# A third seven-product unit pair in the first panel pairs of the down projection, with deeper rings for the weights' parts

## The chip, the cores and the metric

The kernel runs on one core of one Trainium2 chip. The metric is the device time of one execution in microseconds, as a median of several runs. The profile is that of one execution; its span runs from the first to the last instruction. TensorE is called PE, its weight loads PEld, VectorE DVE, ScalarE ACT, GpSimd POOL; SP is the engine that only issues transfers.

## The reference, cut to what matters

Two layers work on 256 tokens of width 2048, in float32. Layer 0 mixes with gated linear attention, layer 1 with forgetting attention; both also attend to 256 memory tokens. Each layer ends in a gated feed-forward network with a causal convolution over three tokens:

```python
def conv_ffn(h, w_up, conv_w, conv_b, w_down):
    u = causal_dwconv(h @ w_up, conv_w, conv_b)      # h: (256, 2048), w_up: (2048, 11264)
    a, val = split_cols(u, [FFN_HIDDEN, FFN_HIDDEN])
    return (jax.nn.silu(a) * val) @ w_down           # w_down: (5632, 2048)
```

The change lies in `@ w_down`, in both layers, and in the buffers that all projections share.

## The kernel before, in words

**Exact products from three.** Every float32 operand is split into a rounded high part and the rest: `hi` by a ScalarE copy to float32r, `lo = raw - hi` by a VectorE subtraction. A product of two operands is then three matmuls: high by high, low by high, high by low. The activations are split once and stay in SBUF (tiles A and B, 16 chunks of 128 features). The weights come from HBM as they are used.

**Units and rings.** A weight panel is 512 output columns wide. It is cut into units of two chunks of 128 inputs, so a unit is a tile of 128 x 1024 values, 512 KB. A unit passes three rings of tiles: `raw` (four tiles, filled by a transfer that SP issues), `whi` (three, written by ScalarE) and `wlo` (three, written by VectorE). A tile is free again when its last reader is done: `raw` after the subtraction, `whi` after its last matmul with the high part, `wlo` after the last with the low part. `split_unit` and `load_unit` (lines 197 to 219) do this for an ordinary unit: line 207 issues the transfer, line 208 casts, line 217 subtracts. `products` (lines 221 to 233) issues its twelve matmuls: two halves of the tokens, two chunks, three products.

**Seven products in place of eight.** `proj_seven` (lines 270 to 370) computes two panels at once. For one place u in the sum, the two chunks, the two token halves and the two panels form a 2 by 2 block product of eight block products; ordinary unit pairs do all eight, 24 matmuls. For the places listed in `forms`, a Strassen-like form needs seven, 21 matmuls. It needs weight sums (`t13`, `t24`, four VectorE operations on lines 346 to 349, one tile each, not doubled), a half tile (`vhi`, `vlo`) and token sums, the "forms", which `token_sums` makes from the activations beforehand. Four of the seven products go to PSUM banks of their own (`ps_t`, two `ps_s`, `ps_o`), and `more` adds them to the residual stream behind the pair. `halves` (line 307) casts (line 314) and subtracts (line 315) for such a unit, `load` fetches its raw tile; both use the same rings. All matmuls of `proj_seven` are issued by `emit` on line 291.

**The feed-forward network** (`ffn`) goes in three parts of 16, 16 and 12 hidden chunks. In a part, the up panels are computed one after the other, each giving two chunks; its result is written to HBM in turned order, read back (tile `u`), passed through the convolution and the gate in `taken`, and split. Then the down projection of the part runs as four panels, in the first two parts as two pairs, each eight places long. `SEVEN` names the places with the seven-product form in the first and the second pair; `LAST` is the same for the third part and empty.

```python
SEVEN = ((3, 5), (3, 5, 7))
...
for f, at in zip((0, 2), SEVEN):
    add_seven(key, f, m, {u: form(forms[u]) for u in at}, spare_tile)
```

Places are counted from 0 here: 3, 5 and 7 are the 4th, 6th and 8th. `taken` makes the forms of the places for which a tile is held, as soon as the place's two chunks are there.

**What sets the order.** The queues' order is chosen while the program is built, by a planner that runs a timeline of its own. Loads, casts and subtractions of weights have priority over the rest (`AHEAD`), so they run ahead of TensorE as far as the rings let them. Steps such as writing, reading back and convolving are counted in units (`later`, `passed`) and stand behind the cast of that unit in ScalarE's order. [...]

Of the kernel before, what the change touches and what calls it, by code (L numbers as in the profile page):

```python
# [12 lines left out]
F32 = mybir.dt.float32  # L13
F32R = mybir.dt.float32r
# [5 lines left out]
P = 128  # L20
# [11 lines left out]
PARTS = ((0, 16), (16, 32), (32, 44))  # L32
# [4 lines left out]
NVER = 96  # L37
NUNIT = 1024
AHEAD = 300
SEVEN = ((3, 5), (3, 5, 7))  # L40
LAST = ()

SPREAD = [128 * q + 32 * k + i for k in range(4) for i in range(32) for q in range(4)]

WARM = 8

FV_PARTS = ((0, 376), (376, 764), (764, 1152), (1152, 1536))

# [89 lines left out]
def _trunk(ctx: ExitStack, tc: tile.TileContext, xt, xtok, memt, wp, wgu, gns, gfin, cnv, par, msk, out):  # L138
    nc = tc.nc
    where, _ = _layout()  # L140
# [3 lines left out]
    wpool = ctx.enter_context(tc.tile_pool(name="wpool", bufs=4))  # L144
# [25 lines left out]
    with tc.high_priority(offset=2 * AHEAD):  # L170
        V.memset(bufB[KC - 1].bitcast(F32), 0.0)
        warm = pwork.tile([P, 512], F32, name="ps_o", tag="o", bufs=1)
        for i in range(WARM):
            TE.matmul(warm, bufB[KC - 1][:, 0, :P], bufB[KC - 1], start=i == 0, stop=i == WARM - 1)

# [7 lines left out]
    def passed():  # L183

        for d in due:
            d[0] -= 1
        for d in [d for d in due if d[0] == 0]:
            due.remove(d)
            with tc.issue_after(casts[-1].ins):
                d[1]()  # L190
# [6 lines left out]
    def load_unit(unit, pieces=1, before=None, pool=wpool):  # L197
        off, kcs, n = unit
        w = len(kcs) * n
        raw = wpool.tile([P, NUNIT], F32, name="raw", tag="raw", bufs=4)  # L200
        hi = pool.tile([P, NUNIT], F32R, name="whi", tag="whi", bufs=3)
        src = wp[off : off + P * w].rearrange("(p n) -> p n", p=P)
        for i in range(pieces):
            if before is not None:
                before(i)
            s = slice(i * w // pieces, (i + 1) * w // pieces)
            loads.append(nc.sync.dma_start(raw[:, s], src[:, s]))
            casts.append(S.activation(hi[:, s], raw[:, s], AF.Copy))  # L208
        return raw, hi, w

    def split_unit(unit, pieces=1, before=None, pool=wpool):
        with tc.high_priority(offset=AHEAD):
            raw, hi, w = load_unit(unit, pieces, before, pool)
            lo = pool.tile([P, NUNIT], F32R, name="wlo", tag="wlo", bufs=3)
            for i in range(pieces):
                s = slice(i * w // pieces, (i + 1) * w // pieces)
                V.tensor_tensor(lo[:, s], raw[:, s], hi[:, s].bitcast(F32), ALU.subtract)  # L217
        passed()
        return hi, lo
# [50 lines left out]
    def proj_seven(keys, src, forms, evacs, tiles, more, early=False):  # L270

        units = [where[k] for k in keys]
        count, n = len(units[0]), units[0][0][2]
        base = min(min(u[1]) for u in units[0])
        acc = [[pacc.tile([P, 512], F32, name="acc", tag="acc") for _ in range(2)] for _ in keys]
        begun, calls = set(), {}
        shared = []

        def form(a, x, hi, lo, c):
            s = slice(c * n, (c + 1) * n)  # L280
            out = []
            for xs, w in ((x[0], hi), (x[1], hi), (x[0], lo)):
                out.append((a, xs, w[:, s]))
            return out

        def emit(groups):
            todo = [g[n] for n in range(2) for g in groups] + [g[2] for g in groups]
            for a, x, w in todo:
                k = id(a)
                calls[k] -= 1  # L290
                TE.matmul(a[:, :n], x, w, start=k not in begun, stop=calls[k] == 0)  # L291
                begun.add(k)

        def count_calls(a, n):
            calls[id(a)] = calls.get(id(a), 0) + n

        plain = [u for u in range(count) if u not in forms]
        for i in range(2):
            for b in range(2):
                count_calls(acc[i][b], 6 * len(plain))  # L300
        for a in (acc[0][0], acc[1][0], acc[0][1]):
            count_calls(a, 3 * len(forms))

        def token(kc, b):
            return [src[kc - base][:, i, b * P : (b + 1) * P] for i in range(2)]

        def halves(raw, single=False):
            w = n if single else 2 * n
            if single:
                hi, lo = (tiles(t, F32R) for t in ("vhi", "vlo"))  # L310
            else:
                hi, lo = (wpool.tile([P, NUNIT], F32R, name=t, tag=t, bufs=3) for t in ("whi", "wlo"))
            hi, lo = hi[:, :w], lo[:, :w]
            casts.append(S.activation(hi, raw, AF.Copy))  # L314
            V.tensor_tensor(lo, raw, hi.bitcast(F32), ALU.subtract)
            return hi, lo

        def load(unit):
            off, kcs, n = unit
            w = len(kcs) * n  # L320
            raw = wpool.tile([P, NUNIT], F32, name="raw", tag="raw", bufs=4)[:, :w]
            loads.append(nc.sync.dma_start(raw, wp[off : off + P * w].rearrange("(p n) -> p n", p=P)))
            return raw

        for u in range(count):
            k0, k1 = units[0][u][1]
            if u not in forms:
                for i in range(2):
                    hi, lo = split_unit(units[i][u])
                    emit([form(acc[i][b], token(kc, b), hi, lo, c) for b in range(2) for c, kc in enumerate((k0, k1))])  # L330
                    if u == count - 1:
                        for b in range(2):
                            evacs[i](b, acc[i][b][:, :n])
                if u == count - 2 and count - 1 in forms:
                    evacs[1](1, acc[1][1])
                continue
            if not shared:
                shared += [work(t, m) for t, m in (("t", 1), ("s", 2), ("o", 1), ("s", 2))]
                for a in shared:
                    count_calls(a, 3 * len(forms))  # L340
            m1, m5, m6, m7 = shared
            s = forms[u]
            with tc.high_priority(offset=AHEAD + 40):
                r0, r1 = (load(units[i][u]) for i in range(2))
                t13, t24 = (tiles(t, F32)[:, : 2 * n] for t in ("t13", "t24"))
                V.tensor_tensor(t13[:, :n], r1[:, :n], r0[:, :n], ALU.subtract)
                V.tensor_tensor(t13[:, n:], r1[:, n:], r1[:, :n], ALU.subtract)
                V.tensor_tensor(t24[:, :n], r1[:, n:], t13[:, :n], ALU.subtract)
                V.tensor_tensor(t24[:, n:], r0[:, n:], t24[:, :n], ALU.subtract)  # L349
            with tc.high_priority(offset=AHEAD):  # L350
                v0 = halves(r0)
                v1 = halves(r1[:, n:], True)
            passed()
            emit([form(m1, token(k0, 0), *v0, 0), form(acc[0][0], token(k1, 0), *v0, 1)])
            emit([form(acc[1][0], s(3), *v1, 0)])
            with tc.high_priority(offset=AHEAD):
                v2 = halves(t13)
            emit([form(m5, s(0), *v2, 0), form(m7, s(2), *v2, 1)])
            with tc.high_priority(offset=AHEAD):
                v3 = halves(t24)  # L360
            passed()
            emit([form(m6, s(1), *v3, 0), form(acc[0][1], token(k1, 1), *v3, 1)])
            if u == count - 1:
                for i, b in ((0, 0), (1, 0), (0, 1)):
                    evacs[i](b, acc[i][b])
            if early and u == max(forms):
                more(m1, m5, m6, m7)

        if not early:
            more(m1, m5, m6, m7)  # L370
# [692 lines left out]
    def ffn(l, nx, h, m, then, ending=None):  # L1063
        with tc.tile_pool(name=f"ffn{l}", bufs=1) as fp, ExitStack() as ends:
# [3 lines left out]
            sp = sums.enter_context(tc.tile_pool(name=f"sums{l}", bufs=1))  # L1068
# [3 lines left out]
            for u in us:  # L1072
                nc.gpsimd.memset(u[:, :, :2], 0.0)
            turn = [0]
            tiles = [sp.tile([P, 2, 4, P], F32R, name=f"forms{i}") for i in range(3)]
            held = []

            def spare_tile(name, dtype):
# [45 lines left out]

                return evac

            parts = {lo: dict(zip(SEVEN[1] if p < len(PARTS) - 1 else LAST, tiles)) for p, (lo, _) in enumerate(PARTS)}
            for p, (lo, hi) in enumerate(PARTS):
                forms = parts[lo]
                js = list(range(lo, hi, 2))  # L1130
# [6 lines left out]
                if p < len(PARTS) - 1:  # L1137
                    for f, at in zip((0, 2), SEVEN):
                        add_seven(key, f, m, {u: form(forms[u]) for u in at}, spare_tile)
# [33 lines left out]
    n, then, _ = preparing("ffn0", bufB)  # L1173
# [4 lines left out]
    n, then, _ = preparing("ffn1", bufA)  # L1178
# [41 lines left out]
    def closing(ends):  # L1220
        op = ends.enter_context(tc.tile_pool(name="store", bufs=1))
        made["y"] = op.tile([P, 2, 512], F32, name="y")
        return op

    ffn(1, n, bufA, bufB, None, (opened, closing))


# [83 lines left out]
```

## Time and profile before

| | |
|---|---|
| median of 3 runs | 2241.3 us (2240.88 to 2243.91) |
| the profiled execution, span | 2241.1 us |
| matmuls | 10267, PE busy 2227.2 us (99%) |
| VectorE, ScalarE busy | 1658.5 us (74%), 1294.0 us (58%) |
| transfers | 516.98 MB, mean 231 GB/s |
| mean granted TensorE clock | 0.999 |

On one core the span is nearly all of an execution: the profiled one lies inside the spread of the timed runs. A line of the groups view reads: source line, engine, operation, tile written <- tiles read, shape, count | busy time, mean ns of one | idle time of the engine just before, and what ended it. A line of the waits reads: who waited <- for whom: us in total, times, longest. A line of a timeline reads: start, length, engine, source line, operation, tiles, count, and in brackets the idle time before and what ended it.

### The profile page before, as it was taken

The numbers are of one execution on the slowest core, as the hardware profiler recorded it, in microseconds if no ns is written. First come the engines' busy times: TensorE is split into PE (matmuls) and PEld (weight loads), VectorE is DVE, ScalarE is ACT, GpSimd is POOL, SyncE is SP. The second block draws the span as 40 slices with busy tenths as digits, with TensorE's granted clock in tenths as the row PEclk, the third lists the DMA queues.
The fourth block names the chain that finished last, engine by engine and source line by source line (L and its number), as shares of the span: only waits on it lengthen the run. The fifth ranks groups of instructions, "written<-read, shape, count | busy, mean of one in ns | idle before, by whom it ended". The sixth has DMA issues, their size and how long they took to land.

```text
span 2241.1 us, 29637 instructions
## 1 busy us (share of the span) xinstructions
PE 2227.2 (99%) x10267; PEld 1860.8 (83%) x10267; DVE 1658.5 (74%) x2608; ACT 1294.0 (58%) x1921; POOL 44.6 (2%) x71
## 2 busy tenths in 40 slices
PE   9999999999999999999999999999999999999998
PEld 7888888888888888888888898888888888888886
DVE  7568887667689677886777875666778967787766
ACT  7555665656565465555656655555665555554654
POOL 0000000000000000000000000000000000000000
PEclk9999999999999999999999999999999999999999
DMA  9875667677875778667778777677876677767784
GB/s 319 277 234 188 205 208 224 202 234 242 256 222 201 243 233 249 213 203 246 235 254 263 243 239 222 196 233 244 255 243 220 204 239 244 240 193 233 237 242 150
DMA packets 276894, 516.98 MB, mean 231 GB/s; under 512 B 149884, under 2 KB 158600, under 8 KB 276616
## 3 DMA queue, kind: packets, MB, share of 16 engines
q1 hardware_dynamic: 124296, 427.24, 58.9%
q10 hardware_dynamic: 149760, 80.51, 12.6%
q0 software_dynamic: 2688, 7.34, 1.1%
q8 instruction: 80, 1.31, 0.2%
q14 instruction: 70, 0.57, 0.1%
HBM read 470.44 MB, written 44.58 MB: 230 GB/s over the span
## 4 chain that ended last, share of the span: by engine, by line
PE 95%; DMA 3%; DVE 1%; issue 1%; ACT 0%; SPq 0%; DVEq 0%; ACTq 0%
PE acc L229 24%; PE acc L230 24%; PE acc L233 24%; PE acc L291 16%; PE ps_s L291 1%; DMA back<-xturned 1%; PE ps_o L291 1%; PE ps_t L291 1%; DMA back<-turned 1%; DMA raw<-wp 1%; PE ps_s L833 0%; DMA turned<-square 0%; PE ps_s L634 0%; PE ps_t L623 0%; PE ps_o L645 0%
## 5 line engine op out<-in xcount | busy, mean ns | idle before, releaser
L217 DVE TENSOR_TENSOR wlo<-raw,whi 128x1024 fp32r<-128x1024 f32 (+4 forms) x763 | 912.6, 1199 | 458.0 <-ACT whi L208 429.5
L208 ACT ACTIVATE whi<-raw 128x1024 fp32r<-128x1024 f32 (+4 forms) x763 | 791.2, 1040 | 704.7 <-PE acc L230 471.9
L229 PE MATMUL acc<-whi,B 128*128 128x512 f32 (+3 forms) x1440 | 548.1, 382 | 0.0
L230 PE MATMUL acc<-whi,B 128*128 128x512 f32 (+3 forms) x1440 | 547.9, 382 | 0.0
L229 PE MATMUL acc<-whi,A 128*128 128x512 f32 x1120 | 437.3, 392 | 1.7 <-ACT whi L208 1.4
L230 PE MATMUL acc<-whi,A 128*128 128x512 f32 x1120 | 435.4, 390 | 0.0
L233 PE MATMUL acc<-wlo,B 128*128 128x512 f32 (+3 forms) x1440 | 377.0, 381 | 0.0
L229 PEld LDWEIGHTS acc<-whi,B 128*128 128x128 f32 x1440 | 270.3, 188 | 46.9
L230 PEld LDWEIGHTS acc<-whi,B 128*128 128x128 f32 x1440 | 269.9, 188 | 46.3
L233 PEld LDWEIGHTS acc<-wlo,B 128*128 128x128 f32 x1440 | 267.7, 188 | 46.4
L233 PE MATMUL acc<-wlo,A 128*128 128x512 f32 x1120 | 300.6, 390 | 0.3 <-DVE wlo L217 0.3
L229 PEld LDWEIGHTS acc<-whi,A 128*128 128x128 f32 x1120 | 210.3, 188 | 48.1 <-ACT whi L208 3.6
L233 PEld LDWEIGHTS acc<-wlo,A 128*128 128x128 f32 x1120 | 210.1, 188 | 44.3 <-DVE wlo L217 0.7
L230 PEld LDWEIGHTS acc<-whi,A 128*128 128x128 f32 x1120 | 210.3, 188 | 43.5 <-DVE A L527 0.2
L291 PE MATMUL acc<-whi,B 128*128 128x512 f32 x508 | 132.2, 390 | 0.0
L291 PE MATMUL acc<-whi,A 128*128 128x512 f32 x496 | 129.9, 390 | 0.0
L291 PEld LDWEIGHTS acc<-whi,B 128*128 128x128 f32 x508 | 95.1, 188 | 20.3
L1092 ACT ACTIVATE cv<-u,cw 128x256 f32<-128x256 f32 x176 | 96.8, 588 | 23.9 <-DMA u<-turned 23.9
L291 PEld LDWEIGHTS acc<-whi,A 128*128 128x128 f32 x496 | 93.1, 188 | 19.9
L314 ACT ACTIVATE whi<-t 128x1024 fp32r<-128x1024 f32 x46 | 48.9, 1062 | 79.2 <-DVE t L349 42.7
L1093 DVE SCALAR_TENSOR_TENSOR cv<-u,cw,cv 128x256 f32<-128x256 f32 x176 | 78.5, 479 | 15.6 <-ACT cv L1092 15.6
L438 DVE STREAM_TRANSPOSE square<-scaled 128x512 f32<-128x512 f32 x122 | 80.3, 692 | 0.0
(259 smaller groups left out, 1819.5 us busy)
## 6 DMA issues: line engine op xcount, KB each, us to landing
raw<-wp SPq DMA_DIRECT2D x743, 512.0 KB, 4.2
turned<-square ACTq DMA_DIRECT2D x61, 512.0 KB, 4.5
u<-turned ACTq DMA_DIRECT2D x176, 128.0 KB, 5.2
raw<-wp SPq DMA_DIRECT2D x32, 384.0 KB, 3.2
raw<-wp SPq DMA_DIRECT2D x24, 388.0 KB, 3.9
xturned<-square ACTq DMA_DIRECT2D x12, 512.0 KB, 4.3
back<-xturned ACTq DMA_DIRECT2D x40, 128.0 KB, 5.6
raw<-wp SPq DMA_DIRECT2D x8, 400.0 KB, 3.8
```

Source lines behind the costliest of these rows:

```text
L208: casts.append(S.activation(hi[:, s], raw[:, s], AF.Copy))
L217: V.tensor_tensor(lo[:, s], raw[:, s], hi[:, s].bitcast(F32), ALU.subtract)
L229: TE.matmul(acc[:, :n], xh, hi[:, s], start=first and j == 0, stop=False)
L230: TE.matmul(acc[:, :n], xl, hi[:, s], start=False, stop=False)
L233: TE.matmul(a, xh, ls, start=False, stop=stop)
L291: TE.matmul(a[:, :n], x, w, start=k not in begun, stop=calls[k] == 0)
L314: casts.append(S.activation(hi, raw, AF.Copy))
L438: V.transpose(self.square[:, :, :, b], src.rearrange("p (c t) -> p c t", t=32))
L1092: S.activation(r, v[:, 2:], AF.Identity, bias=w[3], scale=w[2])
L1093: V.scalar_tensor_tensor(r, v[:, 1 : T + 1], w[1], r, ALU.mult, ALU.add)
```

## The change

The first pair of the first two down parts gets the seven-product form at a third place, index 1, beside 3 and 5; the second pair keeps its three. A fourth tile for token forms is held, and `SUMS` names the places for which forms are made. The rings become five `raw`, four `whi` and four `wlo` tiles for all projections that use the common pool. The scratch area of the transfers that POOL issues is set to 4096 bytes.

```diff
--- before.py
+++ after.py
@@ -37,12 +37,15 @@
 NVER = 96
 NUNIT = 1024
 AHEAD = 300
-SEVEN = ((3, 5), (3, 5, 7))
+SEVEN = ((1, 3, 5), (3, 5, 7))
+SUMS = (1, 3, 5, 7)
 LAST = ()
 
 SPREAD = [128 * q + 32 * k + i for k in range(4) for i in range(32) for q in range(4)]
 
 WARM = 8
+RING = {"raw": 5, "whi": 4, "wlo": 4}
+SCRATCH = 4096
 
 FV_PARTS = ((0, 376), (376, 764), (764, 1152), (1152, 1536))
 
@@ -197,8 +200,8 @@
     def load_unit(unit, pieces=1, before=None, pool=wpool):
         off, kcs, n = unit
         w = len(kcs) * n
-        raw = wpool.tile([P, NUNIT], F32, name="raw", tag="raw", bufs=4)
-        hi = pool.tile([P, NUNIT], F32R, name="whi", tag="whi", bufs=3)
+        raw = wpool.tile([P, NUNIT], F32, name="raw", tag="raw", bufs=RING["raw"])
+        hi = pool.tile([P, NUNIT], F32R, name="whi", tag="whi", bufs=RING["whi"] if pool is wpool else 3)
         src = wp[off : off + P * w].rearrange("(p n) -> p n", p=P)
         for i in range(pieces):
             if before is not None:
@@ -211,7 +214,7 @@
     def split_unit(unit, pieces=1, before=None, pool=wpool):
         with tc.high_priority(offset=AHEAD):
             raw, hi, w = load_unit(unit, pieces, before, pool)
-            lo = pool.tile([P, NUNIT], F32R, name="wlo", tag="wlo", bufs=3)
+            lo = pool.tile([P, NUNIT], F32R, name="wlo", tag="wlo", bufs=RING["wlo"] if pool is wpool else 3)
             for i in range(pieces):
                 s = slice(i * w // pieces, (i + 1) * w // pieces)
                 V.tensor_tensor(lo[:, s], raw[:, s], hi[:, s].bitcast(F32), ALU.subtract)
@@ -309,7 +312,7 @@
             if single:
                 hi, lo = (tiles(t, F32R) for t in ("vhi", "vlo"))
             else:
-                hi, lo = (wpool.tile([P, NUNIT], F32R, name=t, tag=t, bufs=3) for t in ("whi", "wlo"))
+                hi, lo = (wpool.tile([P, NUNIT], F32R, name=t, tag=t, bufs=RING[t]) for t in ("whi", "wlo"))
             hi, lo = hi[:, :w], lo[:, :w]
             casts.append(S.activation(hi, raw, AF.Copy))
             V.tensor_tensor(lo, raw, hi.bitcast(F32), ALU.subtract)
@@ -318,7 +321,7 @@
         def load(unit):
             off, kcs, n = unit
             w = len(kcs) * n
-            raw = wpool.tile([P, NUNIT], F32, name="raw", tag="raw", bufs=4)[:, :w]
+            raw = wpool.tile([P, NUNIT], F32, name="raw", tag="raw", bufs=RING["raw"])[:, :w]
             loads.append(nc.sync.dma_start(raw, wp[off : off + P * w].rearrange("(p n) -> p n", p=P)))
             return raw
 
@@ -1072,7 +1075,7 @@
             for u in us:
                 nc.gpsimd.memset(u[:, :, :2], 0.0)
             turn = [0]
-            tiles = [sp.tile([P, 2, 4, P], F32R, name=f"forms{i}") for i in range(3)]
+            tiles = [sp.tile([P, 2, 4, P], F32R, name=f"forms{i}") for i in range(len(SUMS))]
             held = []
 
             def spare_tile(name, dtype):
@@ -1124,7 +1127,7 @@
 
                 return evac
 
-            parts = {lo: dict(zip(SEVEN[1] if p < len(PARTS) - 1 else LAST, tiles)) for p, (lo, _) in enumerate(PARTS)}
+            parts = {lo: dict(zip(SUMS if p < len(PARTS) - 1 else LAST, tiles)) for p, (lo, _) in enumerate(PARTS)}
             for p, (lo, hi) in enumerate(PARTS):
                 forms = parts[lo]
                 js = list(range(lo, hi, 2))
@@ -1298,7 +1301,7 @@
         "par": par,
         "msk": _constants(),
     }
-    nc = bacc.Bacc("TRN2", target_bir_lowering=False, num_devices=1)
+    nc = bacc.Bacc("TRN2", target_bir_lowering=False, num_devices=1, dynamic_dma_scratch_size=SCRATCH)
     aps = [nc.dram_tensor(n, v.shape, mybir.dt.from_np(v.dtype), kind="ExternalInput").ap()
            for n, v in arrays.items()]
     aps.append(nc.dram_tensor("out", (2, P, D), F32, kind="ExternalOutput").ap())
```

## The prediction

> **What bounds the kernel now.** I read the page first: busy times, slices, the chain of waits.
>
> ```profile
> span 2241.1 us, 29637 instructions
> PE 2227.2 (99%) x10267; PEld 1860.8 (83%) x10267; DVE 1658.5 (74%) x2608; ACT 1294.0 (58%) x1921; POOL 44.6 (2%) x71
> ...
> PE   9999999999999999999999999999999999999998
> PEclk9999999999999999999999999999999999999999
> ...
> PE 95%; DMA 3%; DVE 1%; issue 1%; ACT 0%; SPq 0%; DVEq 0%; ACTq 0%
> ```
>
> TensorE is busy in every slice at the full granted clock, and 95% of the chain is matmuls. A busy PE need not be a PE at its pace, so the second view is PE's own waits, whole list:
>
> ```profile
> PE ps_o L174 <- DVE B L171: 1.5, 1, 1.5
> PE acc L229 <- ACT whi L208: 1.4, 3, 0.7
> PE ps_s L634 <- DMA back<-turned: 1.1, 2, 0.8
> PE acc L233 <- DVE wlo L217: 0.3, 1, 0.3
> PE acc L229 <- ACT A L526: 0.2, 1, 0.2
> ```
>
> 4.5 us in 2241, and none on line 291, the matmuls of the seven-product panels. So time is the number of matmuls times their pace, and a change pays only by issuing fewer of them, so long as casts and subtractions stay ahead. The pace comes from windows cut, on line 291 alone, at the first matmul of a seven-product unit pair and of the plain pair behind it (layer 0, part 0, places 4 and 5):
>
> ```profile
> 659.57:664.43 4.86, 4.86 (x22) 3.94 (x21) 1.00 0.37 122
> 664.43:669.87 5.44, 5.44 (x25) 4.50 (x24) 1.00 0.44 140
> ```
>
> The first column is the stretch and its length, then PE and PEld busy with their counts. The weight loads count 21 and 24 products (PE's x22 and x25 take in the tail of the matmul before). A plain pair takes 5.44 us, 227 ns a product; a seven-product pair 4.86 us, 231 ns a product.
>
> **The change part by part.**
>
> *Third pair at place 2.* SEVEN[0] gains index 1, in parts 0 and 1 of both layers: four places. Each goes from 24 matmuls to 21, and by the two windows from 5.44 to 4.86 us: -0.58 us, together **-2.3 us**. All of it is on the path, as PE waits for nothing there.
>
> [...]
>
> *What it costs VectorE and ScalarE.* By form (the last line is the answer on source line 400):
>
> ```profile
> L217 DVE TENSOR_TENSOR wlo<-raw,whi 128x1024 fp32r<-128x1024 f32 x697 | 850.0, 1222 | 415.5 <-ACT whi L208 393.1 <-PE acc L291 11.5 <-PE acc L233 4.0
> L208 ACT ACTIVATE whi<-raw 128x1024 fp32r<-128x1024 f32 x697 | 735.4, 1058 | 638.8 <-PE acc L230 422.3 <-issue 60.1 <-PE acc L291 47.9
> L315 DVE TENSOR_TENSOR wlo<-t,whi 128x1024 fp32r<-128x1024 f32 x46 | 55.9, 1222 | 15.9 <-ACT whi L314 12.5 <-PE acc L291 3.2
> L314 ACT ACTIVATE vhi<-raw 128x512 fp32r<-128x512 f32 x23 | 14.5, 628 | 18.4 <-DMA raw<-wp 13.4 <-DVE t L346 4.9
> L315 DVE TENSOR_TENSOR vlo<-raw,vhi 128x512 fp32r<-128x512 f32 x23 | 15.8, 685 | 0.5 <-ACT vhi L314 0.5
> L346 DVE TENSOR_TENSOR t<-raw 128x512 f32<-128x512 f32 x23 | 15.9, 691 | 9.5 <-DMA raw<-wp 9.3
> L349 DVE TENSOR_TENSOR t<-raw,t 128x512 f32<-128x512 f32 x23 | 15.8, 685 | 0.0
> L406 DVE TENSOR_TENSOR forms<-sf,forms 128x512 fp32r<-128x512 f32 x15 | 10.3, 687 | 1.8 <-ACT forms L405 1.6
> ...
> L400 DVE TENSOR_TENSOR sf<-cv,cv x12: 283/285/291, 579.9 to 1983.5; 128x128 f32<-128x128 f32 x12
> ```
>
> A plain pair takes VectorE 2 x 1.22 = 2.44 us. A seven-product pair takes four weight sums (L346 to L349, 4 x 0.69), one half tile (0.69) and three full ones (3 x 1.22): 7.1 us. That is +4.66 us in each of the four panel pairs. ScalarE goes from 2 x 1.06 to 3 x 1.06 + 0.63: +1.7 us, on an engine at 58%. The fourth token form costs 4 x 0.29 + 0.69 = 1.8 us of VectorE a part. The first form of now, that of place 4, is made at 579.9; that of place 2 comes from an earlier panel, so over 65 us before its products at 648.7, and lies beside the up projection. No step changes its queue, and the DMA moves the same weights. Whether the 4.66 us hide is the whole question; windows over the first and second panel pair, all engines (PE, PEld, DVE, ACT, POOL):
>
> ```profile
> 643.24:685.69 42.45, 42.45 (x187) 34.91 (x186) 35.07 (x51) 25.69 (x33) 0.00 (x0) 1.00 0.70 221
> 685.69:727.30 41.61, 41.61 (x184) 34.16 (x183) 38.26 (x46) 21.32 (x23) 0.00 (x0) 1.00 0.57 192
> ```
>
> VectorE has 35.07 us of work in the first; it would have 39.73 in 41.87, 95%, against 92% in the second, which already holds three such units and lets PE wait for nothing. The mean hides the order, so I take the lead: when a subtraction ends, and when the product that reads it starts. VectorE and PE in order of time, layer 0 and layer 1:
>
> ```profile
> 671.92 2.36 DVE L315 TENSOR_TENSOR wlo<-t,whi 128x1024 fp32r<-128x1024 f32 x2
> 674.74 0.63 PE L291 MATMUL ps_s<-wlo,forms 128*128 128x512 f32 x2
> 1721.85 2.35 DVE L315 TENSOR_TENSOR wlo<-t,whi 128x1024 fp32r<-128x1024 f32 x2
> 1724.20 0.62 PE L291 MATMUL ps_s<-wlo,forms 128*128 128x512 f32 x2
> ```
>
> The first of the two ends at 671.92 + 1.22 = 673.14, 1.60 us ahead of 674.74; in layer 1 the lead is 1.13. These are the smallest of the first pairs. Taking 4.66 us out of a lead of 1.1 to 1.6, with PE 0.58 us earlier, would leave -3.6 to -4.1. What pays for it is idle time of VectorE just before:
>
> ```profile
> 650.76 1.23 DVE L217 TENSOR_TENSOR wlo<-raw,whi 128x1024 fp32r<-128x1024 f32 x1 [3.13 <-PE acc L291]
> 652.49 0.69 DVE L346 TENSOR_TENSOR t<-raw 128x512 f32<-128x512 f32 x1 [0.50 <-DMA raw<-wp]
> 660.01 1.23 DVE L315 TENSOR_TENSOR wlo<-t,whi 128x1024 fp32r<-128x1024 f32 x1 [1.00 <-ACT whi L314]
> 662.39 0.69 DVE L346 TENSOR_TENSOR t<-raw 128x512 f32<-128x512 f32 x1 [0.76 <-DMA raw<-wp]
> ```
>
> 3.13 + 0.50 + 1.00 + 0.76 = 5.4 us between 647 and 663, right where the new unit's work falls (place 2 is read from 648.7 on). 5.39 is 0.15 more than 4.66 + 0.58, so the lead at 673 would come out about as it is, if the idle time can be used.
>
> *Deeper tiles.* The 3.13 us end on a product that sets a tile free: with four tiles in place of three that wait goes, and casts and subtractions may run one unit further ahead, 12 products or 2.72 us. The fifth raw tile does the same for the two waits on the load. This makes the 5.4 us usable and adds up to 2.72 us. Elsewhere PE gains only the waits on a cast, at most 1.4 us, in three places. Two of them, ScalarE and PE in order of time:
>
> ```profile
> 8.40 1.06 ACT L208 ACTIVATE whi<-raw 128x1024 fp32r<-128x1024 f32 x1 [1.24 <-DMA raw<-wp]
> 9.51 0.50 PE L229 MATMUL acc<-whi,A 128*128 128x512 f32 x1 [0.65 <-ACT whi L208]
> ...
> 1519.22 0.98 ACT L526 ACTIVATE A<-back,gains 128x256 fp32r<-128x256 f32 x2 [2.76 <-DMA back<-xturned]
> 1520.11 1.04 ACT L208 ACTIVATE whi<-raw 128x1024 fp32r<-128x1024 f32 x1
> 1521.21 0.50 PE L229 MATMUL acc<-whi,A 128*128 128x512 f32 x1 [0.54 <-ACT whi L208]
> ```
>
> The first stands behind a load at the start, which no tile makes faster. In the second ScalarE had stood behind a transfer, and the cast came late; one more cast in hand covers that. So 1.4 - 0.65 = 0.8 us bounds the gain; against it, casts run ahead in ScalarE's and VectorE's queues may put a cast and a subtraction (1.06 + 1.22) in front of a step that PE waits for, at the two such places (L634, L526): up to +4.6 us, and PE's present wait there is 1.3. I take zero for both together, nearest to what the rows show PE waiting, and keep -0.8 and +4.6.
>
> *Smaller scratch for POOL's transfers.* The diff sets it to 4096 and shows no former value.
>
> ```profile
> q0 software_dynamic: 2688, 7.34, 1.1%
> ...
> back<-xturned POOLq DMA_DIRECT2D x24, 128.0 KB, 5.8
> ...
> 1154.13 1.49 POOL L446 DMA_DIRECT2D back<-xturned  x2 [13.37 <-DMA xturned<-square]
> 1158.46 1.49 POOL L446 DMA_DIRECT2D back<-xturned  x2 [2.84 <-DMA xturned<-square]
> ```
>
> POOL issues in pairs, 0.75 us apiece and 5.8 us to landing; the densest place has four in flight. If four fit, the cost is nothing. If only one fits, the second of a pair goes out 5 us late, which PE feels where it takes up a stream just turned (the start of each FFN and of the FoX layer, three places): +15 us. I take nothing: 1.1% of the DMA time and POOL busy 2% say that little is queued.
>
> [...]
>
> **Sum.** -2.3 us and zeros: the profiled span of 2241.1 becomes 2238.8. The median shown, 2241.3, is 0.2 from that span, inside the runs' spread (2240.88 to 2243.91); I forecast **2238.8 us**, 0.1% less. Within 0.2% (4.5 us, 2236.8 to 2245.8) a measurement of this kernel hardly tells a change from none.
>
> **Rivals.**
>
> *VectorE becomes the bound of the first panel pair (other side).* If the idle time can't be used, because the new unit's raw tiles come late or the sums queue behind the convolution's steps, PE waits 3.6 us a place in layer 0 and 4.1 in layer 1: 2 x 3.6 + 2 x 4.1 - 2.3 = +13, 2254. It decides once the lead at 673 falls by over 1.60 us (1.13 in layer 1), and the gain is gone at 0.58 us of wait a place. For it: leads thin as they are, 95% load. Against it: the second pair's 92%, and the tile more. In part, 0.3 to 1.5 us a place, it gives 2240 to 2243.
>
> *The rings give more.* The 0.8 us on casts go, and the 1.1 us at L634 and 0.3 at L233 with them: 2238.8 - 2.2 = 2236.6. Against it: L634 waits for a transfer, which no ring shortens.
>
> *POOL's scratch holds transfers back*: +15 us, 2254. Against it: four in flight at most.
>
> *The third unit doesn't shorten the pair*, its products slowed as 231 against 227 ns shows: even twice that loss, 21 x 4 ns, leaves 0.5 us a place, and 2239.2. It is no case of its own.
>
> **How the numbers follow.** Forecast, 2237.6 to 2239.8: 0.58. Rings give more: 0.14, of which 0.09 lie under 2236.8. VectorE waits in part (2239.8 to 2243): 0.17. VectorE in full, POOL or queue order (over 2243): 0.11, of which 0.07 over 2245.8. So faster 0.09, same 0.84, slower 0.07. The range of 8 in 10 is 2236.4 to 2242.4; it leaves out the full starvation and POOL.
>
> **What would show it.** Right: 10255 matmuls; first panel pairs of 41.87 us, as long as the second's; no wait of PE on line 291; VectorE near 39.7 us busy there, the 3.13 us before its second place gone. Wrong: PE waiting for L315 or L314 in the four pairs; first pairs over 42.45 us; POOL waiting between transfers of a pair; new PE waits at L634 or L526.

## The result, and the profile after

| | before | after |
|---|---|---|
| median | 2242.78 us (19 runs, 2240.88 to 2247.37) | 2239.56 us (19 runs, 2237.37 to 2242.6) |
| ratio, 95% interval | | 0.9983 [0.9977, 0.9989] |
| profiled execution, span | 2241.1 us | 2238.8 us |
| matmuls | 10267 | 10255 |

The time falls by 0.17%, and the forecast of 2238.8 us is 0.8 off. A run's time stands 1.8 us over its span (2240.59 beside 2238.8). Times are medians, spans are those of one execution each. The head of the page of after:

```profile
span 2238.8 us, 29733 instructions
PE 2224.6 (99%) x10255; PEld 1859.2 (83%) x10255; DVE 1676.0 (75%) x2652; ACT 1302.4 (58%) x1933; POOL 44.7 (2%) x71
```

Twelve matmuls fewer, TensorE as busy as before. (Three lines were added above; before's 208, 217, 291, 314 and 349 are now 211, 220, 294, 317 and 352.) PE's waits, whole list:

```profile
PE acc L232 <- ACT whi L211: 1.5, 2, 0.8
PE ps_o L177 <- DVE B L174: 1.5, 1, 1.5
PE ps_o L294 <- ACT whi L317: 0.9, 2, 0.6
PE ps_s L637 <- DMA back<-turned: 0.7, 1, 0.7
PE acc L232 <- ACT A L529: 0.2, 1, 0.2
```

The third line is new: seven-product matmuls now wait for a cast, as none did before (0.56 us at 1721 in a first pair, 0.32 at 1244 in another projection that uses the form). Windows of after over the first and second panel pair of layer 0, part 0, then the three other first pairs (PE, PEld, DVE, ACT, POOL):

```profile
642.33:684.40 42.07, 42.07 (x184) 34.22 (x183) 41.14 (x60) 27.19 (x36) 0.00 (x0) 1.00 0.73 235
684.40:726.15 41.75, 41.75 (x184) 34.37 (x183) 38.02 (x46) 21.90 (x24) 0.00 (x0) 1.00 0.56 195
900.23:942.05 41.82, 41.82 (x185) 34.37 (x183) 40.10 (x59) 26.82 (x35) 0.00 (x0) 1.00 0.71 231
1690.80:1733.52 42.72, 42.16 (x185) 34.22 (x183) 41.28 (x60) 27.08 (x36) 0.00 (x0) 1.00 0.71 231
1949.36:1991.31 41.95, 41.95 (x184) 34.21 (x183) 41.00 (x59) 27.10 (x36) 0.00 (x0) 1.00 0.71 236
```

Only one of the four first pairs has the expected 41.8 us. The third is longer than before the change (42.72 against 42.43 to 42.45). In sum the four are 168.6 us against 169.8 before, -1.2 and not -2.3; the other 1.1 us of the span's -2.3 came from elsewhere. VectorE is busy 40.1 to 41.3 us there, 96 to 98%. What happened in the third, VectorE, ScalarE and PE in order of time:

```profile
1714.38 0.68 DVE L351 TENSOR_TENSOR t<-raw,t 128x512 f32<-128x512 f32 x1
...
1719.18 0.68 DVE L352 TENSOR_TENSOR t<-raw,t 128x512 f32<-128x512 f32 x1
...
1719.97 1.06 ACT L317 ACTIVATE whi<-t 128x1024 fp32r<-128x1024 f32 x1 [3.47 <-DVE t L352]
...
1721.09 0.50 PE L294 MATMUL ps_o<-whi,forms 128*128 128x512 f32 x1 [0.56 <-ACT whi L317]
```

The last weight sum starts only 4.8 us after the one before it: between them VectorE makes three subtractions (line 318, 3.1 us), two steps of the last up panel's convolution (line 1097, 0.47 us each), a sum of a token form and the end of a split. ScalarE waits 3.47 us for it, PE 0.56 for the cast.

### The profile page after: what moved, and what is told of

It reads as the page before. It is cut to its first block, busy times and chain, and to the rows that moved or that the text cites. A ratio compares the mean times of both kernels' runs of the same rounds, so it can differ in the third digit from the quotient of the medians.

```text
span 2238.8 us, 29733 instructions
## 1 busy us (share of the span) xinstructions
PE 2224.6 (99%) x10255; PEld 1859.2 (83%) x10255; DVE 1676.0 (75%) x2652; ACT 1302.4 (58%) x1933; POOL 44.7 (2%) x71
## 4 chain that ended last, share of the span: by engine, by line
PE 97%; DMA 2%; DVE 1%; ACT 0%; issue 0%; SPq 0%; ACTq 0%; DVEq 0%
PE acc L232 25%; PE acc L233 25%; PE acc L236 25%; PE acc L294 15%; PE ps_s L294 2%; PE ps_o L294 1%; PE ps_t L294 1%; DMA back<-xturned 1%; DMA back<-turned 0%; PE ps_s L836 0%; PE ps_t L626 0%; PE ps_s L637 0%; PE ps_o L648 0%; DMA raw<-wp 0%; PE ps_s L1009 0%; PE ps_o L856 0%
## 5 line engine op out<-in xcount | busy, mean ns | idle before, releaser
L220 DVE TENSOR_TENSOR wlo<-raw,whi 128x1024 fp32r<-128x1024 f32 (+4 forms) x755 | 897.3, 1197 | 427.2 <-ACT whi L211 400.6
L211 ACT ACTIVATE whi<-raw 128x1024 fp32r<-128x1024 f32 (+4 forms) x755 | 776.8, 1037 | 612.2 <-PE acc L233 302.3
L1095 ACT ACTIVATE cv<-u,cw 128x256 f32<-128x256 f32 x176 | 99.8, 593 | 41.3 <-DMA u<-turned 40.9
L317 ACT ACTIVATE whi<-t 128x1024 fp32r<-128x1024 f32 x54 | 57.2, 1061 | 53.4 <-PE acc L294 34.1
```

The lines of the kernel that those rows point to most:

```text
L1095: S.activation(r, v[:, 2:], AF.Identity, bias=w[3], scale=w[2])
```

## Experiments

Each kernel was timed in turns with the kernel before on one chip; kernels under one heading shared the runs of before. A kernel has ten or eleven runs, third pair only has five. Theory A: time is the number of products, the rings only keep casts ahead. Theory B: the rings themselves bring the gain.

### The two halves of the change, and two other choices of places

| kernel | matmuls | ratio to before | median (before 2244.06) | runs from, to | span |
|---|---|---|---|---|---|
| rings only | 10267 | 0.998 [0.9971, 0.9988] | 2239.37 | 2238.89, 2240.34 | 2238.1 |
| third pair only | 10255 | 1.0035 [1.0023, 1.0048] | 2251.78 | 2248.87, 2254.35 | 2249.6 |
| four places in the second pair | 10243 | 1.0005 [0.9995, 1.0014] | 2244.06 | 2241.74, 2252.31 | 2239.8 |
| places 1, 3, 7 in the first pair | 10255 | 0.9975 [0.9966, 0.9985] | 2238.37 | 2236.31, 2241.35 | 2238.0 |

*Rings only.*

```diff
-SEVEN = ((1, 3, 5), (3, 5, 7))
-SUMS = (1, 3, 5, 7)
+SEVEN = ((3, 5), (3, 5, 7))
+SUMS = (3, 5, 7)
```

> Rings of five and four tiles and the scratch of 4096 as in the change, but the seven-product places of before (3 and 5, counted from 0, in the first pair; a form is made for 3, 5 and 7). Theory A (time is the number of products; the rings only keep the casts and subtractions ahead): 10267 matmuls, first pairs of 42.45 us, and at most the 0.8 us of PE's waits on casts are gained: 0 to -0.8 us against before, ratio 0.9996 to 1.0. Theory B (the rings themselves bring what the change brings, by waits and steps all over the kernel): -2.5 to -3.2 us, ratio near 0.9985.

Theory B: the span falls by 3.0 us without one product fewer, and the median by 4.7 (2244.06 to 2239.37), more than either theory said. This kernel keeps the change's scratch of 4096; so do five raw tiles only, below, which gain 1.3 us in the median and can't be told from before, so the scratch isn't what brings the rest. First its busy line on the page:

```profile
PE 2225.2 (99%) x10267; PEld 1861.5 (83%) x10267; DVE 1656.0 (74%) x2608; ACT 1295.5 (58%) x1921; POOL 44.8 (2%) x71
```

PE's waits, whole list, where no wait on a seven-product matmul stands:

```profile
PE ps_o L177 <- DVE B L174: 1.5, 1, 1.5
PE acc L232 <- ACT whi L211: 0.9, 1, 0.9
PE ps_s L637 <- DMA back<-turned: 0.7, 1, 0.7
PE acc L232 <- ACT A L529: 0.4, 1, 0.4
```

And its window over the first pair of layer 0, part 0:

```profile
641.34:683.75 42.41, 42.41 (x187) 34.91 (x186) 37.34 (x53) 25.62 (x33) 0.00 (x0) 1.00 0.70 234
```

The pair itself is as long as before (42.45), but it starts 1.9 us earlier (641.34 against 643.24). Of these, 1.7 us come in one stage, from 378 to 417 us, where layer 0's memory attention meets its output projection. Before, PE waited there:

```profile
384.23 1.13 PE L634 MATMUL ps_s<-mk,back 128*128 128x256 f32 x4 [0.84 <-DMA back<-turned]
388.35 0.50 PE L229 MATMUL acc<-whi,A 128*128 128x512 f32 x1 [0.24 <-ACT whi L208]
```

With the deeper rings PE has no wait between 378 and 417, so 1.1 of the 1.7 us are these two waits. Of the 1.1 us of span gained behind the pair's start, some 0.8 come around 1520, where before's wait of 0.54 us on a cast is gone; the rest is small, with parts of either sign. The stage from 378 to 417 isn't safe, though: of the eleven profiled executions with four whi tiles ten gain 1.5 to 1.7 us there, and the change in its second profile (in the last table) loses 0.7.

*Third pair only.*

```diff
-RING = {"raw": 5, "whi": 4, "wlo": 4}
-SCRATCH = 4096
+RING = {"raw": 4, "whi": 3, "wlo": 3}
+SCRATCH = 16384
```

> The third seven-product pair at index 1 with the rings of before (four raw, three whi, three wlo) and a scratch of 16384. Theory A: 10255 matmuls, but VectorE's 3.13 us of waiting for a free tile can't be used, so of 4.66 + 0.58 us only the lead of 1.1 to 1.6 us and 2.3 us of other idle time pay: PE waits 1.4 us a place in layer 0 and 1.9 in layer 1, +6.5 - 2.3 = +4 us against before. Rival (the rings aren't needed): PE waits no more than in the changed kernel, -2.3 us, ratio 0.999.

Slower, by more than expected. Windows over its four first pairs:

```profile
643.57:687.81 44.24, 42.41 (x184) 34.13 (x183) 40.29 (x59) 26.99 (x36) 0.00 (x0) 1.00 0.65 213
903.68:949.54 45.86, 44.03 (x184) 35.30 (x183) 39.33 (x57) 26.48 (x35) 0.00 (x0) 0.96 0.64 206
1698.92:1742.26 43.34, 42.30 (x184) 34.12 (x183) 39.44 (x57) 26.44 (x35) 0.00 (x0) 1.00 0.66 214
1958.16:2002.12 43.96, 42.44 (x184) 34.12 (x183) 39.74 (x58) 26.57 (x35) 0.00 (x0) 1.00 0.63 212
```

And two of PE's waits there:

```profile
PE ps_o L294 <- ACT whi L317: 4.2, 4, 1.0
PE ps_s L294 <- DVE wlo L318: 2.0, 3, 0.8
```

Against 41.87 they lose 2.4, 4.0, 1.5 and 2.1 us: VectorE as the bound of the first pair. PE's waits on line 294 are 1.8, 1.8, 1.0 and 1.5 us of that, in sum near the expected 1.4 and 1.9 a place and about half the prediction's price of 3.6 to 4.1. The second pair loses some 1.7 us more to the clock, which stood at half behind its two waits:

```profile
936.50:939.90 3.40, 3.40 (x9) 2.73 (x9) 3.40 (x6) 2.65 (x4) 0.00 (x0) 0.50 0.41 128
```

*Four places in the second pair*: SEVEN = ((1, 3, 5), (1, 3, 5, 7)).

> The change, and index 1 in the second panel pair too, so it has four seven-product places (1, 3, 5, 7); its form is held already. 10243 matmuls. Theory A: another 4 x 0.58 = -2.3 us against the changed kernel, if the lead that VectorE has at the start of the second pair (about 5 us) pays for 38.7 + 4.66 = 43.4 us of work in 41.85: -5 us or a little more against before, ratio 0.9975. Rival (VectorE is the bound of a pair with over three such places): PE waits on line 294 for casts and subtractions, 0.5 us or more a pair, and the time is that of the changed kernel or longer.

The rival holds, at another spot. The second pairs do get shorter (41.4 us in three of four), but PE waits in front of them, for VectorE to add the first pair's sums to the stream (4.3 us in the four); layer 0, part 0:

```profile
684.13 1.16 PE L294 MATMUL acc<-whi,A 128*128 128x512 f32 x4 [1.20 <-DVE x L1038]
```

*Places 1, 3, 7*: SEVEN = ((1, 3, 7), (3, 5, 7)).

> The change with index 7 in place of 5 in the first pair (1, 3, 7), so that the third unit isn't under VectorE at the same time as the convolution of the last up panel. 10255 matmuls. Theory A (VectorE was late at index 5, where the second weight sum stood behind the convolution's steps and the cast waited 3.47 us): the waits of 0.86 us in the first pair of layer 1, part 0 and 0.26 in layer 0, part 0 go, first pairs of 41.9 us everywhere, about -1 us against the changed kernel, ratio 0.9980 against before. Rival (the form of index 7, made from the last panel, is late instead): PE waits for the forms at the start of the eighth place, 0.5 us or more a pair.

In layer 0 both first pairs took 41.77 us, with no wait: the form of index 7 is in time. In layer 1 they took 43.43 and 43.08, for a wait at the first unit, index 1, that no theory had named:

```profile
1693.20 1.18 PE L294 MATMUL ps_s<-whi,forms 128*128 128x512 f32 x4 [1.34 <-ACT whi L317]
```

### Which ring, the scratch, and a later convolution

| kernel | ratio to before | median (before 2242.85) | runs from, to | span |
|---|---|---|---|---|
| five raw tiles only, old places | 0.9994 [0.9985, 1.0002] | 2241.56 | 2240.8, 2242.69 | 2239.8 |
| four whi and wlo only, old places | 0.9989 [0.998, 0.9998] | 2239.77 | 2239.01, 2244.51 | 2238.1 |
| the change, scratch 1024 | 0.9988 [0.9979, 0.9997] | 2239.37 | 2237.4, 2248.1 | 2237.1 |
| the change, later convolution | 0.9982 [0.9974, 0.9991] | 2239.37 | 2237.15, 2243.63 | 2235.3 |

*Five raw tiles only*: RING = {"raw": 5, "whi": 3, "wlo": 3}, SEVEN and SUMS as in rings only.

> The seven-product places of before, five raw tiles, but three whi and three wlo as before, scratch 4096. The four rings together took 3.0 us off one profiled execution and narrowed the runs to 2238.9 to 2240.3. Theory C (the casts' and subtractions' tiles did it: ScalarE waits 470 us for products to set a whi tile free and only 27 us for loads): -0.5 to +0.5 us against before, and the runs spread as wide as before's (some 5 us). Theory D (the fifth raw tile did it, by taking up the transfers' jitter): ratio 0.998, runs within 2 us.

*Four whi and wlo only*: RING = {"raw": 4, "whi": 4, "wlo": 4}, SEVEN and SUMS as in rings only.

> The seven-product places of before, four raw tiles as before, but four whi and four wlo, scratch 4096. Theory C: ratio 0.998 as with all rings, the stage of layer 0's memory attention (378 to 417 us) shorter by 1.5 us, runs within 2 us. Theory D: 1.0.

Theory C for the mean: the parts' tiles bring 3 us of span, as much as all rings, and 1.7 of them from 378 to 417 us. Theory D is half right: the raw tile can't be told from nothing by its interval, but its 11 runs lie within 1.9 us, where before's 33 spread over 5.5 (standard deviation 0.5 against 1.2 us); with the parts' tiles alone one run of 11 reached 2244.51. Neither theory had expected that split.

*Scratch 1024*: SCRATCH = 1024.

> The changed kernel with the scratch of POOL's transfers at 1024 bytes in place of 4096. If the scratch bounds how many of POOL's transfers are in flight, and 4096 was enough for the four seen at once, a quarter of it should make POOL's busy time grow or its second transfer of a pair go out late (5 us apart in place of 0.75), and cost up to 15 us. If POOL never waits for room, the time is the changed kernel's (ratio 0.998 against before).

POOL's pairs do come apart; its timeline:

```profile
1150.12 0.75 POOL L449 DMA_DIRECT2D back<-xturned  x1 [15.27 <-DMA xturned<-square]
1154.14 0.76 POOL L449 DMA_DIRECT2D back<-xturned  x1 [3.27 <-issue]
1159.60 0.75 POOL L449 DMA_DIRECT2D back<-xturned  x1 [4.70 <-issue]
```

Before, two went out in 1.49 us; now there are 4.0 and 5.5 us between one and the next. The row of POOL's waits on that (in total, times, longest):

```profile
POOL back L449 <- issue: 100.5, 22, 10.5
```

The changed kernel's list at 4096 has one, of 10.7 us, and before's has one of 10.9 beside two short ones; so some 90 us in 21 waits are new here. POOL's other transfers (qk, fkt, mk) add 39.7 us in nine: some 130 us in 30 waits, 4.3 each in the mean. And the time is the changed kernel's: PE doesn't feel it. At 4096 bytes two still go out in 1.49 us (at 1151.99 and 1157.42 in the changed kernel), and such a transfer took 6.4 us to land there (median of 24; 5.8 before). How many of them fit in 1024 or 4096 bytes isn't shown.

*Later convolution.*

```diff
-                    proj_tm(("up", l, j), h, panel(j, lo))
+                    proj_tm(("up", l, j), h, panel(j, lo, 2 if p < 2 and j == js[-1] else 0))
```

> The change, but the convolution steps of a part's last up panel (first two parts) stand two units later (10 and 11 units behind the panel in place of 8 and 9), so behind the weight sums of index 5 in VectorE's queue. Theory A (the third unit pays 0.58 us a place once VectorE isn't late): PE's waits of 0.9 us on line 317's casts go, first pairs of 41.87 us, about -1.3 us against the changed kernel, ratio 0.9977 against before. Rival (VectorE has 40.2 us of work in 41.9 us and is late wherever the convolution stands): PE still waits 0.5 us or more in the first pairs, and the time is the changed kernel's.

This profiled execution is theory A to the letter: 2235.3 us, no wait on line 294, and four first pairs of

```profile
640.87:682.71 41.84, 41.84 (x185) 34.36 (x184) 39.61 (x58) 27.44 (x36) 0.00 (x0) 1.00 0.70 222
898.56:940.40 41.84, 41.84 (x185) 34.36 (x184) 39.88 (x58) 27.06 (x35) 0.00 (x0) 1.00 0.72 228
1688.24:1730.12 41.88, 41.88 (x184) 34.27 (x183) 41.00 (x60) 27.58 (x36) 0.00 (x0) 1.00 0.72 237
1946.00:1987.80 41.80, 41.80 (x185) 34.35 (x184) 39.38 (x57) 27.00 (x35) 0.00 (x0) 1.00 0.70 234
```

But it was the fastest of eleven runs (2237.15), and the median is no better than that of the rings alone on the other chip. So the third unit had to be weighed on one chip.

### What the third unit is worth

| kernel | ratio to before | median (before 2243.47) | runs from, to | span |
|---|---|---|---|---|
| later convolution, no third unit | 0.9982 [0.9973, 0.9991] | 2239.43 | 2238.92, 2240.45 | 2238.6 |
| the change | 0.9983 [0.9974, 0.9992] | 2239.22 | 2237.6, 2242.61 | 2238.9 |
| later convolution, sums on POOL | 0.9998 [0.9989, 1.0007] | 2242.32 | 2239.87, 2248.29 | 2243.5 |
| later convolution | 0.998 [0.9971, 0.9989] | 2238.94 | 2237.09, 2242.69 | 2239.5 |

*Later convolution, no third unit*: the diff of the later convolution, SEVEN and SUMS as in rings only.

> Rings of the change, the convolution of a part's last up panel two units later, but the seven-product places of before (3 and 5 in the first pair). Against the run with the third unit and the later convolution on the same chip it says what the third unit is worth where VectorE isn't late. Theory A: 10267 matmuls, 0.58 us a place slower than with the third unit: +2.3 us, and about 2239.4 us (the rings alone). Rival (the later convolution itself brought the time, the third unit nothing): the same time as with the third unit.

*The change again.*

> The changed kernel as it is, on the same chip as the three others. Theory A: its third unit pays 2.3 us in an execution in which VectorE is in time and less where it is late, so its median lies between those of the kernels with and without the third unit at the later convolution, and its runs spread wider (5 us) than with the old places (1.5 us).

Median and spread (5.0 us) come as expected. But its profiled execution (2238.9 us) isn't one in which VectorE is late: no wait stands on line 294, and the four first pairs take 168.0 us against 169.4 without the third unit. The loss lies elsewhere, at the memory attention, in layer 0 and, with 0.84 us at 1324, in layer 1:

```profile
384.98 1.13 PE L637 MATMUL ps_s<-mk,back 128*128 128x256 f32 x4 [2.16 <-DMA back<-turned]
```

PE's order up to there is that of rings only, where this wait was gone, and the four reads back were issued by 379.2 us, 0.6 earlier than there. So the transfer itself came late, and part of the spread isn't the third unit's.

*Later convolution again.*

> The change with the later convolution, as run before, beside the same without the third unit. Theory A: 2.3 us under it in an execution in which VectorE is in time (a first pair of 41.8 us against 42.4), and 1 to 2.3 us under it in the median. Rival: no difference in the median.

The rival holds in the median: with the third unit 0.2 us (the change) and 0.5 us (later convolution) less than without, inside every interval. Theory A holds for the best execution: 2237.1 against 2238.9, -1.8 us. The worst is 2242.7 against 2240.5. With the unit the runs scatter more. The same kernel in two executions shows one way; layer 0, part 0, first the window of the execution of 2239.5 us (called late here), then its wait on PE:

```profile
640.93:684.77 43.84, 42.08 (x184) 34.31 (x183) 42.11 (x64) 27.93 (x37) 0.00 (x0) 1.00 0.67 217
```

```profile
646.49 1.20 PE L294 MATMUL ps_s<-whi,forms 128*128 128x512 f32 x4 [1.76 <-ACT whi L317]
```

ScalarE's timeline ahead of it in the late one:

```profile
625.54 0.34 ACTq L444 DMA_DIRECT2D turned<-square  x1
631.05 1.53 ACTq L449 DMA_DIRECT2D u<-turned  x3
...
638.67 0.63 ACT L317 ACTIVATE vhi<-raw 128x512 fp32r<-128x512 f32 x1 [0.59 <-DMA raw<-wp]
```

And in the execution of 2235.3 us:

```profile
623.20 0.34 ACTq L444 DMA_DIRECT2D turned<-square  x1
628.17 1.68 ACTq L449 DMA_DIRECT2D u<-turned  x3
...
635.95 0.64 ACT L317 ACTIVATE vhi<-raw 128x512 fp32r<-128x512 f32 x1 [0.70 <-DMA raw<-wp]
```

PE starts the pair at the same time (640.93 and 640.87), but the cast of the first seven-product unit starts 2.7 us later in the late one. 2.3 us of it stood there when the last up panel but one was written (625.54 against 623.20); from the write's issue to the read's it is 5.5 against 5.0 us, and ScalarE stands still meanwhile. The lag begins 130 us ahead, on ScalarE, with the issue of an earlier panel's write. First the execution of 2235.3 us, then the late one:

```profile
515.05 0.46 ACTq L444 DMA_DIRECT2D turned<-square  x1
```

```profile
514.49 2.77 ACTq L444 DMA_DIRECT2D turned<-square  x1
```

This issue takes 0.34 us in the median; here it held ScalarE for 2.77. From there to the pair ScalarE's weight casts start 1.1 to 4.5 us behind those of the other execution, where they had been at most 0.3 behind since 300 us, while PE stays within 0.1 us. PE feels it only at the third unit, where it waits 1.76. Why the issue took so long, and whether it alone keeps the lag alive, isn't shown.

*Sums on POOL*: `token_sums` of the feed-forward network with `nc.gpsimd.tensor_tensor` for its four sums.

> The change with the later convolution, and the four sums of each token form of the feed-forward network (4 x 0.29 us) on POOL in place of VectorE. Theory A (VectorE's lateness in the first pairs is what spreads the runs): 1.1 us less of VectorE's work in a first pair, no wait of PE on line 294, 0 to -1 us against the kernel with the later convolution alone, and a narrower spread. [...]

Theory A fails: the median is 3.4 us over the later convolution's (2242.32 and 2238.94), and the runs spread wider (8.4 against 5.6 us). PE waits on casts at index 1 in layer 1's first pairs (0.92 and 1.50 us, then 1.36). POOL takes 0.5 to 1.4 us for a sum that takes VectorE 0.29, in the means by source line. VectorE's subtractions keep their length (1226 ns against 1223). All four first pairs together grow to 174.4 us, and PE is busy 2227.1 us with the 10255 matmuls that took 2224.6 in the change's first profile. Why the casts are late isn't shown.

```profile
L404 POOL TENSOR_TENSOR sf<-cv 128x128 f32<-128x128 f32 x16 | 22.3, 1395 | 821.4 <-DVE cv L1100 821.4
```

No version beats the change beyond its interval; places 1, 3, 7 and the later convolution have the lowest medians and the lowest single runs.

## Why the prediction was right, and where not

The time lay in the range, and the change is under 0.2% as forecast; but the sum's two terms were each wrong, and cancelled. So the number was luck more than insight.

- **The rings, taken at zero, are the whole gain.** The step "I take zero for both together" failed, and with it the bound of 0.8 us. It was read off the waits on casts alone. Those two waits (0.24 at 388, 0.54 at 1521) did go, as the prediction allowed; but the rings alone gave -3.0 us of span, and a ratio of 0.998 with the old places. The prediction held that no ring shortens the wait at the memory attention, as it is for a transfer. Ten of eleven profiled executions with four whi tiles are without that wait in layer 0; with the old rings it was 0.84 us, and 1.44 in third pair only. In the eleventh the transfer came late and PE waited 2.16, so the objection stands for such an execution. With the deeper rings PE's order differs from 48 us on, as the planner works anew; whether depth or the new order brings the gain is open.
- **The third unit's -2.3 us, "all of it on the path", is worth 0.2 to 0.5 us in the median**, which isn't told from nothing. The product count (10255), the unit's length and the 41.87 us of a first pair were right, and are seen when VectorE is in time. What failed is the lead: idle time of 5.39 us against 5.24 us of need was taken as cover. The margin of 0.15 us was a single execution's, and such executions differ by 2.7 us at this very place.
- **VectorE's load** was forecast as 39.7 us in a first pair; it was 40.1 to 41.3. The rings alone bring 37.3 where there were 35.1, as 1.3 us of subtractions and 1.3 us of additions to the stream more lie in the window. The later convolution brought it to 39.4 to 41.0.
- **The rival of VectorE as the bound** was right in mechanism and about twice too dear: without the rings PE waits 1.0 to 1.8 us a place, against 3.6 to 4.1. With them it is the case given 0.17, in part of the places and executions: 0.56 us once in the change's first profile, none in its second. The sum given for that case was off: 1.5 us a place is 2244.8, not 2243.
- **POOL's scratch** was rightly priced at nothing. The +15 us of its rival is wrong even where the mechanism runs: at 1024 bytes 30 more transfers wait 4.3 us each in the mean, and PE waits no longer for it.
- **The base.** The prediction put the median 0.2 us from the span. With more runs, before's median is 2242.8 to 2244.1, and a run is 1.8 over its span. So the fall was 3.2 us where 2.5 was forecast.

## What to carry to other kernels

A change with two parts is to be priced in parts by their own rows, also the part that is only there to enable the other: here a deeper buffer alone brought what both brought together. An engine at 95% in a stage, as VectorE was forecast here, can be the bound of that stage in some executions: the first cast of the third unit started 2.7 us later in one execution of a kernel than in another, and VectorE was busy 96 to 98% of the first pairs; saved matmuls count there only as far as the lead covers that shift. And a single profile has one draw of that shift: compare spreads, not only medians.

## What the runs showed of the hardware

The issue of one transfer on ScalarE, 0.34 us in the median of 73, took 2.77 us once, and 110 to 125 us later the casts stood 2.1 to 2.8 us behind those of another execution. In third pair only the granted clock stood at half for 3.4 us (936.50 to 939.90), right behind two waits of PE (0.8 and 1.0 us); the two such pairs of waits in its first and fourth first pair were not followed by it (granted clock 1.00 over both pairs). POOL took 0.5 to 1.4 us in the mean for a strided sum of 128x128 that VectorE does in 0.29. With a scratch of 1024 bytes 30 more of POOL's transfers waited than with 4096, 4.3 us each in the mean. With a fifth raw tile 11 runs lay within 1.9 us, where before's 33 spread over 5.5, with a median only 1.3 us lower.
